# Two rows of conditioning stored another way, and a second, earlier call that makes the first layer's filter spectra

## The chip, the cores and the metric

The kernel runs on one core of a Trainium2 chip. The metric is the device time of one execution in microseconds (us); the median of three runs is compared. An execution is also recorded by the hardware profiler, and all rows below come from that one record.

## The reference, cut to what matters

Two layers of a diffusion backbone. Each layer mixes tokens in four head groups and then applies an MLP. What matters here is the start of the first layer:

```python
mx = modulation(c, ada_w[l], ada_b[l])        # silu(c) @ w + b, six vectors of 1024
mc = modulation(c_ctx, ada_w[l], ada_b[l])    # the same for the 256 context tokens
hx = rmsnorm(x, norm_pre_mix[l]) * (1.0 + mx[1]) + mx[0]
px = hx @ w_in[l]                             # 512 tokens; pc likewise for the context
h_fwd, h_bwd = hyena_filters(L, ...)          # needs weights alone, neither x nor c
y = irfft(rfft(u, n=2*L) * rfft(kern))        # long convolution with that filter, L = 512 and 256
```

The spectrum of the filter (`rfft(kern)`) and the sum of its absolute values depend on weights only. The reference needs each of them once per layer and length.

## The kernel before

All inputs lie in HBM. Almost every transfer is issued by SyncE's queue, SP, which issues in order: an instruction that waits holds all behind it. The order on each engine is fixed when the program is built, by a planner that takes the instructions of the source in turn and lets later ones go ahead where its own cost table finds the earlier ones not ready.

The start, in `run`, goes through these steps. `ccT` brings both conditioning vectors, features on partitions, and SiLU is applied to it. Two transfers store the vectors to a scratch tensor `cdr` in HBM, so that `cond_rows` can later read them back as rows on all 128 partitions (`cbc`). `first_scale` loads six blocks of 128 tokens (`X`, 512 KB each), squares and scales them. `mod_first` multiplies the vectors with four blocks of modulation weights, `adaP`: blocks 0 and 2 first (sixteen loads of 256 KB), blocks 1 and 3 inside the loop below (four loads of 1 MB). `first_turn` puts features on partitions. `filters` runs the small filter network. A loop over two halves of the features (`k0` is 0, then 4) applies the modulation in `first_norm` and gives `acth` and `actl`, the two parts of every main operand.

Then `mix` begins. `hyena_project` makes the main products of the first six blocks of `w_in` (lines 138 to 140; weights come as `raw` and are split into `whi` and `wlo`). Between them, `spectra_at` makes the filter spectra, length 512 ahead of the third block and length 256 ahead of the fifth:

```python
ld = {L: self.spectrum_loads(0, L, fp) for L in DFT_LENS}                            # L1589
self.fp, self.sp_in = fp, [(top[L == 256], ld[L], 0, L) for L in DFT_LENS]           # L1590
```

`spectrum` is a chain: products with the last filter weights (L465, TensorE), the window (L466, VectorE), absolute values (L467, ScalarE), one reduction over all of them (L469, VectorE), the sum and the difference of both directions (L472 and L473, GpSimd, into the buffer `ha` that the reduction has just read), the cosine and sine products (L508 for length 512, L521 for 256), their additions (L512 to L530, VectorE), the norm (L478 to L482) and a store of the spectrum to HBM (L484). The buffers `hw`, `ha`, `hw4`, `win`, `dft` exist once per length or once in all.

Of the kernel before, what the change touches and what calls it, by code (L numbers as in the profile page):

```python
# [9 lines left out]
F32 = mybir.dt.float32  # L10
# [35 lines left out]
class Net:  # L46
# [24 lines left out]
    def setup(self):  # L71
# [7 lines left out]
        # minus one on one block of 32 or 64 partitions  # L79
# [50 lines left out]
    def split(self, x, y, r):  # L130
        """x as two parts, into the columns r of the pair y."""
        self.nc.scalar.copy(y[0][:, r], x)
        self.nc.vector.tensor_sub(y[1][:, r], x, y[0][:, r].bitcast(F32))

    def mm3(self, o, st, mv, first, last):
        """o (+)= st.T @ mv with both operands as sums of two parts."""
        mmul = self.nc.tensor.matmul
        mmul(o, st[0], mv[0], start=first, stop=False)  # L138
        mmul(o, st[0], mv[1], start=False, stop=False)  # L139
        mmul(o, st[1], mv[0], start=False, stop=last)  # L140

    def pair(self):
        """Two banks of PSUM."""
        return self.pb.tile([128, 2, 512], F32, tag="pb", name="pb", bufs=3)

    def big(self, wsrc, acts, segs):
        """Products of one block of output features; returns a PSUM tile per token range."""
# [19 lines left out]
    def mod_first(self, p, i, act, cb=None):  # L167
        """One block of the shift (i < 2) or scale of the first norm. Few rows: four parts of the sum share the
        array's columns. The weights of some blocks lie where the normed activations will go."""
# [29 lines left out]
    def first_scale(self, XS, p):  # L199
        """Each block of 128 features of the input: features onto partitions, in place, with unit norms."""  # L200
# [39 lines left out]
    def cond_rows(self, p):  # L240
        """The activated conditioning vectors as rows on every partition."""
# [5 lines left out]
    def mod_steps(self):  # L247
        """One step per block of rows."""
# [19 lines left out]
    def ring(self, p, tag, bufs):  # L268
        """Where the blocks of modulation weights are loaded from now on."""
        self.row_block = lambda: p.tile([128, D], F32, tag=tag, name="adrow", bufs=bufs)  # L270
# [6 lines left out]
    def fac_pre(self, l, i, cnd, k0=0, k1=KB):  # L277
        """gain * (1 + m) of the norm before a sub-layer; i = 0 mixing, 1 mlp."""
# [4 lines left out]
    def fac_post(self, l, i, cnd, p):  # L283
        """gain * m of the norm after a sub-layer, as a row on every partition."""
# [21 lines left out]
    def post_norm(self, Y, row, X, out, p):  # L306
        """out = X + norm(Y) * gain * m for one block of tokens; returns what ends it, which returns a free buffer."""
# [14 lines left out]
    def finish(self, t, mm, ws, Y, row, X, p, before):  # L322
        """The last products and norm of one block of tokens, by halves of the features; before() ends the block
        before. Returns what ends this one."""
# [23 lines left out]
    def pre_scale(self, X, t, p):  # L348
        """The identity times the reciprocal norms."""
# [5 lines left out]
    def pre_norm(self, l, i, xs, p, out, off, cnd, dgs=None):  # L355
        """Features onto partitions; h = norm(x) * gain * (1 + m) + m' as two parts."""
# [59 lines left out]
    def filters(self, ld, p):  # L416
        """The filter networks up to their last hidden layer, two side by side on the partitions: both layers' of the
        long filter, and both halves of the short one's times."""
# [19 lines left out]
    def spectrum_loads(self, l, L, p):  # L438
        """What a filter's spectrum is made from."""
# [10 lines left out]
    def spectrum(self, hs, ld, l, L, p):  # L450
        """Spectrum of a two-sided filter at the odd frequencies and the norm of each channel."""
# [35 lines left out]
    def spectra(self, dft, uc, us, L, p, sp):  # L487
        """The cosine and sine sums over the even and odd times, E +- O, at the odd frequencies:
        [128 k, (C+, C-, S+, S-), k block, channel]. The frequencies of the second block mirror those of the first:
        there the sums over the times 1 and 3 modulo 4 trade cosines for sines, the others only signs."""  # L490
# [5 lines left out]
        if nk == 2:  # L496
            # (source, cosines or sines, parity, where the sum and the difference go)
# [39 lines left out]
    def hyena_project(self, l, w_in, hx, segs, p):  # L537
        """The convolved projections: x1 * v (two blocks) and x0 (two blocks)."""
# [21 lines left out]
    def hyena(self, l, u, x0, segs, ydst, p):  # L560
        nc, a = self.nc, self.a
        for off, L in segs:
# [43 lines left out]
            # the sums of both blocks that belong to each residue of the time: [(residue, cosine or sine)]  # L606
# [25 lines left out]
    def gdn_project(self, l, nm, j0, w_in, hx, segs, psum):  # L632
        """One of q, k and v: projected, convolved, activated and turned to tokens on partitions."""
# [18 lines left out]
    def gdn_rates(self, l, w_ab, hx, segs, p):  # L652
        """The logs of decay and beta, tokens on partitions. Few columns: four groups of them share the array,
        each with its part of the sum."""
# [27 lines left out]
        def rates(after):  # L682
# [6 lines left out]
            # log(1 + e) = log(w) + (e - (w - 1)) / w with w = fl(1 + e)  # L689
# [13 lines left out]
    def gdn_normalise(self, tok, p, rates):  # L703
        """Unit norm and rotary of keys and queries in place."""
# [44 lines left out]
    def gdn_solve(self, l, tok, la, lbeta, p, values):  # L749
# [3 lines left out]
        # feature-major q and k: [2 heads x 64, pair, tokens]  # L753
# [13 lines left out]
        # cumulative log decay, forward and backward, and the total of each block  # L767
# [47 lines left out]
    def gdn_systems(self, kT, qT, nq, p, ip):  # L815
        """Per direction, block and head: the system's strictly triangular part, transposed, and the query
        weights."""
# [35 lines left out]
    def gdn_inverse(self, UX, p, ip):  # L853
        """UX holds N (strictly triangular parts and a diagonal that is ignored); becomes (I + N)^-1."""
        nc = self.nc
        # the diagonal 32-blocks; slots without a system still pass through the 32 x 32 transposes
# [5 lines left out]
        for dr in range(2):  # L862
# [6 lines left out]
            # the blocks with rows before columns for the first direction, after for the second: both lower  # L869
            nc.vector.transpose(S[:, dr] if dr == 0 else S[:, dr].rearrange("p j i -> p i j"),  # L870
                                G[:, dr].rearrange("p u i -> p i u"))
        # the blocks between the halves go apart, zeros in their place and on the diagonal
# [9 lines left out]
        # substitution inside the 32-blocks, both directions at once  # L882
# [7 lines left out]
        # back: G[32 b + j, u, i] = T[i, j] and its transpose GT  # L890
# [11 lines left out]
    def gdn_levels(self, UX, G, GT, Xt, BB, ip):  # L902
        """From the inverses of the 32-blocks to those of 64 and of 128. Every sum runs over all partitions, with
        zeros in all but one block, which keeps the array at its full clock; the directions and blocks work on
        different columns of it at the same time."""
# [4 lines left out]
        def lower(zp, w, signs):  # L910
            """The products of one stage, negated; a part per block of partitions."""
# [11 lines left out]
        # 32 -> 64: block (a, b) of each pair  # L923
# [38 lines left out]
        # 64 -> 128  # L962
# [25 lines left out]
    def gdn_chain(self, dr, X, qk, ring, tok, seen, nq, p):  # L988
        """The blocks of one direction in turn; yields between stages, so that two directions can alternate.
        The sum of both directions takes the place of the queries."""  # L990
# [13 lines left out]
        def decayed(st):  # L1004
            """Keys and queries times their decay from the start of the block, features on partitions."""
# [109 lines left out]
    def na_project(self, w_in, hx, segs, full, dst):  # L1115
        """Queries and keys as two parts, and the values; one step per block of output features."""
# [26 lines left out]
    def na_heads(self, l, src, y, p, pn, with_ctx):  # L1143
# [7 lines left out]
        for pr in range(2):  # L1151
# [3 lines left out]
            # per head: both parts of the queries, and the keys' first part against each; the keys' second part  # L1155
            # lies with the queries' first
# [26 lines left out]
            for n in range(nq):  # L1183
# [40 lines left out]
                # the heads share the array's columns  # L1224
# [59 lines left out]
    def mix(self, l, hx):  # L1284
# [17 lines left out]
        with self.pool("tok") as self.tp:  # L1302
# [12 lines left out]
            with self.pool("gdn") as gp:  # L1315
# [9 lines left out]
                with self.pool("psg", 4, space=PSUM) as self.pg, self.pool("pso", space=PSUM) as self.po:  # L1325
                    na = self.na_project(w_in[14:20], hx, segs, full, nad)

                    def others(n):
                        """Work that fills the gaps of the inverse, and the values."""
# [28 lines left out]
    def mlp(self, l, ysp, ysp_s):  # L1358
# [7 lines left out]
        def runs(ts):  # L1366
            """Neighbouring tiles with the same modulation."""
# [177 lines left out]
    def run(self):  # L1545
# [11 lines left out]
        with self.pool("x0") as p:  # L1557
            self.cvec = p.tile([128, KB, 32], F32, tag="ccT", name="ccT")
            nc.sync.dma_start(self.cvec, a["ccT"])
            nc.scalar.activation(self.cvec, self.cvec, AF.Silu)  # L1560
            self.cdr = self.dp.tile([1, 2, D], F32, name="cdr", tag="cdr")
            for i in range(2):
                nc.sync.dma_start(self.cdr[0, i].rearrange("(k p) -> p k", p=128), self.cvec[:, :, i])
            fl = self.filter_loads(fp)

            XS = p.tile([128, NBLK, D], F32, name="X0", tag="X0")
            self.first_scale(XS, p)
            for i in (0, 2):
                self.mod_first_out(p, i, self.mod_first(p, i, True))
# [4 lines left out]
            for k0 in (0, 4):  # L1574
                for c in range(2):
                    self.fac_pre(0, 0, c, k0, k0 + 4)
                if k0 == 0:
                    ps = {i: self.mod_first(p, i, False, cb) for i in (1, 3)}
# [4 lines left out]
                if k0 == 0:  # L1583
                    for i in (1, 3):
                        self.mod_first_out(p, i, ps[i])
            nc.sync.dma_start(self.hsd, top[0][64:128])
# [47 lines left out]
def _blocks(w, nb):  # L1634
    """[K, N] -> [N / 128, 128, K / 128, 128]: one contiguous tile per block of outputs."""
# [4 lines left out]
def _layout(x, c, ctx, c_ctx, ada_w, ada_b, norm_pre_mix, norm_post_mix, norm_pre_mlp, norm_post_mlp,  # L1640
# [4 lines left out]
    A["ccT"] = np.pad(np.stack([c[0], c_ctx], -1), ((0, 0), (0, 30))).reshape(KB, 128, 32).transpose(1, 0, 2)  # L1645
    A["adaP"] = ada_w[0][:, :2 * D].reshape(2, 4, 128, 4, 512).transpose(3, 0, 2, 1, 4)
# [28 lines left out]
    # relative position bias, gathered for the queries (row, column) of a column block and its key window  # L1675
# [34 lines left out]
```

## Time and profile before

| what | value |
|---|---|
| median of three runs | 1896.51 us (1891.33 to 1897.97) |
| span of the profiled execution, first to last instruction | 1898.1 us |
| TensorE busy over the span | 1804.4 us, 95% |
| VectorE, ScalarE, GpSimd busy | 1269.1, 775.0, 256.7 us |
| moved by DMA | 233.54 MB, mean 123 GB/s |

The page gives no other time of the profiled execution than its span. Engines are PE (TensorE), PEld (its weight loads), DVE (VectorE), ACT (ScalarE), POOL (GpSimd) and SP. A row of a table by stretch reads: stretch, length, then for PE, PEld, DVE, ACT and POOL the busy time and in brackets the number of instructions, then the granted TensorE clock (1.00 is 2.4 GHz, 0.50 is 1.2 GHz), the busy share of the DMA engines and GB/s. A row of the timeline reads: start, duration, engine, line, operation, output<-input, shapes, count, and in square brackets the idle time before and what ended it. A row of a group reads: line, engine, operation, names, shapes, count, then busy us and mean ns, then idle us before it and what ended that. A row of DMA issues ends with KB each and the median us to landing.

### The profile page before, as it was taken

The page shows a single profiled execution, that of the slowest core. Times are in us where ns is not written, and L with a number is a line of the kernel's source. Part 1 is how long each engine was busy: PE and PEld are TensorE (multiplying, and loading weights), DVE is VectorE, ACT ScalarE, POOL GpSimd, SP SyncE. Part 2 cuts the span into 40 slices and gives each one's busy share as a digit, 9 for nine tenths or more (in the row PEclk, how much of TensorE's full clock was granted, in tenths as well). Part 3 has the DMA queues.
Part 4 walks back from the last instruction along what each step waited for, and adds up shares of the span by engine and source line. Part 5 has one row for each costly group of instructions (what it writes and reads, how often), then busy time and mean ns, then how long its engine had stood idle before and what let it go on. Part 6 is the DMA issues. An engine that isn't in the chain of part 4 may idle for free. (4 is left out here: it accounts for less than half of the span.)

```text
span 1898.1 us, 29470 instructions
## 1 busy us (share of the span) xinstructions
PE 1804.4 (95%) x11170; PEld 1450.4 (76%) x11170; DVE 1269.1 (67%) x2366; ACT 775.0 (41%) x1547; POOL 256.7 (14%) x265
## 2 busy tenths in 40 slices
PE   5899888999999999999999999998899999999998
PEld 2577777777779888888888876777676788777876
DVE  3888989665766777755555586779856665454545
ACT  4433553366556222222222263363346563332323
POOL 0202441500022000000000041152230110000002
PEclk9999999999999999999999999989999999999999
DMA  8452312344555434444434233112233664232322
GB/s 276 145 177 83 121 42 98 120 134 129 166 181 180 146 116 127 131 125 128 133 124 132 78 130 131 62 64 84 77 98 112 194 198 127 83 117 72 106 89 83
DMA packets 107073, 233.54 MB, mean 123 GB/s; under 512 B 14929, under 2 KB 19859, under 8 KB 105652
## 3 DMA queue, kind: packets, MB, share of 16 engines
q1 hardware_dynamic: 106932, 231.67, 38.7%
q8 instruction: 88, 1.44, 0.3%
q14 instruction: 53, 0.43, 0.1%
HBM read 208.41 MB, written 23.21 MB: 122 GB/s over the span
## 5 line engine op out<-in xcount | busy, mean ns | idle before, releaser
L126 ACT CAST whi<-raw 128x512 fp32r<-128x512 f32 x444 | 273.6, 620 | 671.6 <-PE pb L140 261.8
L127 DVE TENSOR_TENSOR wlo<-raw,whi 128x512 fp32r<-128x512 f32 x444 | 316.9, 720 | 215.9 <-ACT whi L126 209.7
L140 PE MATMUL pb<-acth,wlo 128*128 128x512 f32 (+2 forms) x808 | 282.6, 350 | 0.0
L139 PE MATMUL pb<-actl,whi 128*128 128x512 f32 (+2 forms) x808 | 282.2, 349 | 0.0
L138 PE MATMUL pb<-acth,whi 128*128 128x512 f32 (+2 forms) x808 | 281.4, 348 | 0.0
L138 PE MATMUL pb<-whi,hid 128*128 128x512 f32 x628 | 249.6, 397 | 0.1
L139 PE MATMUL pb<-wlo,hid 128*128 128x512 f32 x628 | 248.7, 396 | 0.5 <-DVE wlo L127 0.4
L140 PE MATMUL pb<-whi,hid 128*128 128x512 f32 x628 | 248.6, 396 | 0.0
L1497 DVE TENSOR_TENSOR acc<-acc,pb 128x1024 f32<-128x1024 f32 x96 | 117.2, 1221 | 150.5 <-PE pb L140 149.5
L258 DVE SCALAR_TENSOR_TENSOR junk<-adrow,cbc 128x512 bf16<-128x512 f32 x256 | 181.1, 707 | 5.1 <-DMA adrow<-in_adaD_dram 1.8
L139 PE MATMUL mx<-actl,whi 128*128 128x512 f32 x416 | 174.3, 419 | 1.4 <-POOL actl L374 1.1
L138 PE MATMUL mx<-acth,whi 128*128 128x512 f32 x416 | 170.3, 410 | 2.1 <-ACT acth L235 1.2
L140 PE MATMUL mx<-acth,wlo 128*128 128x512 f32 x416 | 171.7, 413 | 0.5 <-DVE wlo L127 0.4
L138 PEld LDWEIGHTS pb<-acth,whi 128*128 128x128 f32 x808 | 152.5, 189 | 20.3
L139 PEld LDWEIGHTS pb<-actl,whi 128*128 128x128 f32 x808 | 152.1, 188 | 20.1
L140 PEld LDWEIGHTS pb<-acth,wlo 128*128 128x128 f32 x808 | 152.5, 189 | 19.7
L374 POOL TENSOR_TENSOR actl<-et,acth 128x256 fp32r<-128x256 f32 (+2 forms) x64 | 56.1, 892 | 745.1 <-DVE et L373 740.4
L138 PEld LDWEIGHTS pb<-whi,hid 128*128 128x128 f32 x628 | 117.7, 187 | 32.4 <-ACT hid L1398 5.1
L140 PEld LDWEIGHTS pb<-whi,hid 128*128 128x128 f32 x628 | 117.8, 188 | 29.5 <-DVE hid L1399 1.8
L139 PEld LDWEIGHTS pb<-wlo,hid 128*128 128x128 f32 x628 | 117.8, 188 | 28.7 <-DVE wlo L127 1.6
L138 PEld LDWEIGHTS mx<-acth,whi 128*128 128x128 f32 x416 | 79.9, 192 | 20.1 <-ACT acth L235 1.6
L139 PEld LDWEIGHTS mx<-actl,whi 128*128 128x128 f32 x416 | 80.5, 194 | 19.1 <-POOL actl L374 1.8
(396 smaller groups left out, 3033.7 us busy)
## 6 DMA issues: line engine op xcount, KB each, us to landing
raw<-in_w_dram SPq DMA_DIRECT2D x276, 256.0 KB, 2.9
adrow<-in_adaD_dram SPq DMA_DIRECT2D x80, 512.0 KB, 3.7
raw<-in_win_dram SPq DMA_DIRECT2D x104, 256.0 KB, 2.8
raw<-in_wout_dram SPq DMA_DIRECT2D x64, 256.0 KB, 3.0
X<-xdr SPq DMA_DIRECT2D x14, 512.0 KB, 4.6
X<-in_xin_dram SPq DMA_DIRECT2D x12, 512.0 KB, 4.4
xdr<-X SPq DMA_DIRECT2D x10, 512.0 KB, 2.9
adp<-in_adaP_dram SPq DMA_DIRECT2D x16, 256.0 KB, 5.4
```

The costliest lines, as they stand in the source:

```text
L126: self.nc.scalar.copy(hi, raw)
L127: self.nc.vector.tensor_sub(lo, raw, hi.bitcast(F32))
L138: mmul(o, st[0], mv[0], start=first, stop=False)
L139: mmul(o, st[0], mv[1], start=False, stop=False)
L140: mmul(o, st[1], mv[0], start=False, stop=last)
L258: nc.vector.scalar_tensor_tensor(self.junk, raw[:, hs], 1.0, self.cbc[:, cnd, hs], op0=OP.mult, op1=OP.mult, accum_out=self.part[:, l, cnd ...
L374: nc.gpsimd.tensor_sub(lo[:, r], t, hi[:, r].bitcast(F32))
L1497: op = nc.vector.tensor_add(o, o, ps)
```

## The change

The two stores of `cdr` from `ccT`, whose access order `(k p) -> p k` writes single 4-byte elements, are taken out. A new input `ccF` holds the same vectors as 128 rows of 16 values (64 bytes); it is loaded, goes through SiLU, and is stored to `cdr` as 128 rows of 64 bytes, behind the six loads of `X`. The loads of the filter network come first.

In the loop, `spectrum_loads` for both lengths is called ahead of the loads of `adaP` blocks 1 and 3, and `spectrum` is called at the end of each half: length 512 after the first, 256 after the second. Lines 1589 and 1590 and the calls in `hyena_project` are not in the diff: they stay. The rest of the diff takes out comments and leaves blank lines.

```diff
             nc.scalar.activation(self.cvec, self.cvec, AF.Silu)
+            fl = self.filter_loads(fp)
             self.cdr = self.dp.tile([1, 2, D], F32, name="cdr", tag="cdr")
-            for i in range(2):
-                nc.sync.dma_start(self.cdr[0, i].rearrange("(k p) -> p k", p=128), self.cvec[:, :, i])
-            fl = self.filter_loads(fp)
+            flat = p.tile([128, 16], F32, tag="ccF", name="ccF")
+            nc.sync.dma_start(flat, a["ccF"])
+            nc.scalar.activation(flat, flat, AF.Silu)
 
             XS = p.tile([128, NBLK, D], F32, name="X0", tag="X0")
             self.first_scale(XS, p)
+            nc.sync.dma_start(self.cdr[0].rearrange("c (p j) -> (c p) j", j=16), flat)
...
                 if k0 == 0:
+                    ld = {L: self.spectrum_loads(0, L, fp) for L in DFT_LENS}
                     ps = {i: self.mod_first(p, i, False, cb) for i in (1, 3)}
...
                 if k0 == 0:
                     for i in (1, 3):
                         self.mod_first_out(p, i, ps[i])
+                L = DFT_LENS[k0 > 0]
+                self.spectrum(top[L == 256], ld[L], 0, L, fp)
             nc.sync.dma_start(self.hsd, top[0][64:128])
             self.cond_rows(cb)
             self.mods = self.mod_steps()
             ld = {L: self.spectrum_loads(0, L, fp) for L in DFT_LENS}
...
+    A["ccF"] = np.stack([c[0], c_ctx], 0).reshape(128, 16)
```

## Rows read from the trace of the kernel before

**Rows 1.** The page, busy time of each engine over the span.

```profile
PE 1804.4 (95%) x11170; PEld 1450.4 (76%) x11170; DVE 1269.1 (67%) x2366; ACT 775.0 (41%) x1547; POOL 256.7 (14%) x265
```

**Rows 2.** Table by stretch, the input loads (columns are explained above).

```profile
9.00:10.00 1.00, 0.07 (x2) 0.00 (x0) 0.67 (x2) 0.27 (x1) 0.00 (x0) 1.00 1.12 7
...
18.00:19.00 1.00, 0.00 (x0) 0.00 (x0) 0.76 (x4) 0.00 (x0) 0.00 (x0) 1.00 0.27 53
...
18.00:46.00 28.00, 21.35 (x86) 8.44 (x87) 13.38 (x35) 17.77 (x35) 0.00 (x0) 1.00 1.00 386
```

**Rows 3.** DMA view of 6 to 18 us: packets by size, and an issue.

```profile
DMA packets 2400, 0.99 MB, mean 83 GB/s; under 512 B 2112, under 2 KB 2112, under 8 KB 2400
...
cdr<-ccT SPq DMA_DIRECT2D x2, 4.0 KB, 11.0
```

**Rows 4.** Timeline of the first 65 us, ScalarE's rows.

```profile
20.86 1.06 ACT L206 ACTIVATE x0j<-X 128x1024 bf16<-128x1024 f32 x1 [4.15 <-DMA X<-in_xin_dram]
...
48.28 4.91 ACT L235 ACTIVATE acth<-X,mod,fac 128x512 fp32r<-128x512 f32 x8
...
62.11 4.90 ACT L235 ACTIVATE acth<-X,mod,fac 128x512 fp32r<-128x512 f32 x8 [7.38 <-DVE fac L280]
```

**Rows 5.** Table by stretch, from the turned input to the norm's end.

```profile
30.00:48.00 18.00, 17.35 (x87) 7.60 (x84) 10.16 (x26) 10.74 (x23) 0.00 (x0) 1.00 1.02 402
48.00:75.00 27.00, 23.56 (x133) 15.67 (x134) 20.07 (x41) 13.47 (x23) 7.51 (x8) 1.00 0.62 210
```

**Rows 6.** Timeline, products of the spectra at the full clock.

```profile
110.34 1.13 PE L465 MATMUL fps<-hw,hs 64*128 64x512 f32 x4
...
95.75 1.89 PE L508 MATMUL dps<-ha,dft 128*128 128x256 f32 x8
```

**Rows 7.** Groups between 75 and 128 us: the instructions of the spectra.

```profile
L508 PE MATMUL dps<-ha,dft 128*128 128x256 f32 x24 | 8.6, 502 | 3.9 <-POOL ha L472 3.0 <-POOL ha L473 0.8
...
L521 PE MATMUL dps<-ha,dft 128*128 128x256 f32 x8 | 4.1, 638 | 2.9 <-POOL ha L472 2.9
L478 PE MATMUL fps<-cst,hn 128*128 128x1 f32 x8 | 1.2, 252 | 0.0
...
L466 DVE TENSOR_TENSOR hw<-fps,win 128x512 f32<-128x512 f32 x6 | 4.0, 682 | 0.0
...
L481 DVE TENSOR_SCALAR inv<-fps 128x2 f32<-128x2 f32 x2 | 0.3, 148 | 0.0
...
L472 POOL TENSOR_TENSOR ha<-hw 128x1024 f32<-128x1024 f32 (+1 forms) x2 | 5.4, 2706 | 42.0 <-PE mx L138 26.3 <-DVE hn L469 15.7
L473 POOL TENSOR_TENSOR ha<-hw 128x1024 f32<-128x1024 f32 (+1 forms) x2 | 4.5, 2248 | 0.0
```

**Rows 8.** Table by stretch, around both spectra.

```profile
85.00:88.00 3.00, 0.03 (x1) 0.03 (x1) 3.00 (x3) 0.00 (x0) 2.80 (x2) 1.00 0.32 87
...
89.00:95.00 6.00, 5.19 (x14) 3.74 (x13) 5.45 (x10) 1.26 (x3) 1.67 (x1) 0.50 0.32 89
...
117.00:119.00 2.00, 0.00 (x0) 0.00 (x0) 1.97 (x5) 0.00 (x0) 2.00 (x1) 0.97 0.20 43
...
120.00:125.00 5.00, 5.00 (x12) 3.89 (x12) 2.28 (x8) 0.37 (x1) 1.33 (x1) 0.50 0.38 147
```

**Rows 9.** Timeline, the same VectorE subtraction without and beside GpSimd's sums.

```profile
59.77 1.28 DVE L127 TENSOR_TENSOR wlo<-raw,whi 128x512 fp32r<-128x512 f32 x2
...
85.04 6.17 DVE L127 TENSOR_TENSOR wlo<-raw,whi 128x512 fp32r<-128x512 f32 x3
```

**Rows 10.** Timeline of SP's queue from 30 to 70 us.

```profile
33.03 2.37 SPq L181 DMA_DIRECT2D adp<-in_adaP_dram  x4
...
59.15 0.33 SPq L245 DMA_DIRECT2D cbc<-cdr  x1
...
65.27 1.76 SPq L118 DMA_DIRECT2D raw<-in_win_dram  x3
```

**Rows 11.** DMA view of 0 to 80 us: modulation blocks 1 and 3.

```profile
adp<-in_adaP_dram SPq DMA_DIRECT2D x4, 1024.0 KB, 8.9
```

## The prediction

> **What bounds the kernel now.** First comes the page's list of busy times: TensorE is busy 95% of the span [rows 1]. The reader is to see that time can be won only where TensorE waits, starts late or runs at a lower clock, and that work added to TensorE anywhere else is paid in full. All that the change touches lies ahead of 137 us, so I read the table by stretch there. Before 30 us TensorE is nearly idle and the inputs set the pace; from 30 to 75 us it is busy 17.35 of 18 and 23.56 of 27 us [rows 5]; later it stops twice, for the filter spectra [rows 8]. The groups and the timeline then give prices. After 137 us nothing is edited; TensorE stays the bound there, so I carry every microsecond of the front to the end unchanged.
>
> **Part 1, the stores of the conditioning vectors.** From 9 to 19 us the DMA engines are busy but move almost nothing: ten rows of one microsecond, of which the first has 7 and the last 53 GB/s; together they moved some 0.3 MB [rows 2]. In that time 2112 packets under 512 bytes went through, 2048 of them the single elements of the two stores, which took 11.0 us to land [rows 3]. The input blocks lie in the same queue, and ScalarE's second square waits for its block until 20.86 us [rows 4]. Without the stores, 0.3 MB at the 386 GB/s of the later stream [rows 2] takes 0.8 us: 9.2 us are won. The new load and store have 256 packets; at ten microseconds for 2048 that is 1.2 us, of which the load, half, lies ahead of the inputs: 0.6 us. The store and its wait for SiLU stand behind the six loads; behind it in SP's queue are the sixteen weight loads, which wait for the stream anyway. The new SiLU is one small ScalarE instruction in a stretch in which ScalarE waits for data. I take 8.6 us, with 7 and 9.2 as ends. The first norm starts at 48.28 us [rows 4]; it should come that much earlier, since TensorE is packed from 30 us on [rows 5] and the weights that it reads ride in the same stream.
>
> **Part 2, the early spectra.** The diff adds a call and takes none away: lines 1589 and 1590 stay, and so do the calls among the main products. Every spectrum of the first layer is therefore made twice, and both old stops stay where they are. The added work, each instruction at its price:
>
> TensorE: four L465 products take 1.13 us and eight L508 products 1.89 us at the full clock [rows 6], so 0.28 and 0.24 us each. Twelve L465 make 3.4 us, 24 L508 5.7 us, the 8 of L521, the same shape, 1.9 us, and L478 1.2 us [rows 7]. Sum 12.2 us.
>
> VectorE: 13 groups from L466 with 4.0 us to L481 with 0.3 us [rows 7], in sum 18.6 us. GpSimd: 5.4 and 4.5, so 9.9 us [rows 7]. ScalarE gets the absolute values and the copies; it is busy 13.47 of 27 us from 48 to 75 us [rows 5], which hides them.
>
> DMA: eight loads of 2.1 MB in all, now ahead of modulation blocks 1 and 3; at 386 GB/s that is 5.4 us [rows 2]. Those blocks were issued from 33.03 us over 2.37 us [rows 10] and landed after 8.9 us [rows 11], so by about 45 us, but the second half of the norm that needs them came only at 62.11 us [rows 4], behind main products of the first half. The delay of 5.4 us is less than the lead: I cost it at nothing; without the lead it would be 5.4 us. The second set of loads refills buffers that the early set has to release, behind `cbc`, which was issued at 59.15 us [rows 10]; there is no work between that they could hold up but the `raw` weights, below.
>
> What hides the 12.2 us? TensorE's free time from 48 to 75 us, 27 less 23.56, so 3.4 us [rows 5]; 8.8 us are left. If all of it is used and the 0.65 us free between 30 and 48 as well, 8.1 us; if none, 12.2 us.
>
> New waits: the products L508 need GpSimd's sums, and these the long reduction. At the old places TensorE stood still for 3.0 us, later 0.8 us, and 2.0 us in the second table row for this, and after it the clock stood at 0.50, which is 1.2 GHz, for 5.2 and 5.0 us of work, half of which, 5.1 us, is loss [rows 8]. That bounds the early waits between nothing and 10.9 us. The early place has a less loaded VectorE, 20.07 of 27 us against 3.00 of 3 and 5.45 of 6 at the old one [rows 5, 8], so the reduction should come sooner; I take the shorter of the two plain waits, 2.0 us.
>
> SP's queue: the early stores of the spectra wait for the end of their chains, and refills and then the `raw` weights stand behind them. Before, three of these were issued at 65.27 us [rows 10], with the weights of the first two blocks long loaded. I take nothing, with 5.4 us, the time of one set of refills, as the other end.
>
> Sum along TensorE: -8.6 + 8.8 + 2.0 = +2.2 us. Sum along VectorE: it has 6.9 us free from 48 to 75 us [rows 5], so -8.6 + 18.6 - 6.9 = +3.1 us. The two run side by side and the longer one counts: +3 us. From the profiled span of 1898.1 us that is 1901.1 us. The median of the runs stands 1.6 us below the span, so I forecast 1899.5 us: no change that can be told.
>
> **The rivals.**
>
> *The old stop twice (slower).* The place is the wait of L508 and L521 for GpSimd at the end of each half of the norm. If main products of the first half are used up by then, TensorE has nothing to put in between, and both stops with their low clock come again: -8.6 + 8.8 + 10.9 = +11.1 us, 1907.6 us. It decides once more than some 9 of the 10.9 us return. For it: in the old place there were main products ready and the fixed order still stopped. Against it: from 48 to 75 us the clock stayed at 1.00 despite short waits [rows 5].
>
> *VectorE becomes the bound (slower).* Beside GpSimd's sums, three subtractions took 6.17 us where two took 1.28 [rows 9], so 4.2 us more; the sums of the long filter, over half of the 9.9 us, took some 5.5. In the early place the norm's own subtractions lie beside 9.9 us of them: 4.2 x 9.9 / 5.5 = 7.6 us, and +3.1 + 7.6 = +10.7 us, 1907.2 us. It decides once the norm's second half waits for the stretched instructions. Against it: the planner may put the sums beside other work. The Trainium skill (GPSIMD Engine Reference, Key points) says that GpSimd shares its SBUF interfaces with VectorE and contends with VectorE instructions that have two SBUF inputs; the stretched subtraction is one, and no rule there says how much is lost.
>
> *All hidden (faster).* If the planner spreads the early set over TensorE's waits before and inside the norm, and the norm of the second half stays where the weights put it, only part 1 is left: -8.6 us, 1887.9 us. Against it: only some 4 us are free on TensorE [rows 5].
>
> *Only one set is run (faster).* Nothing reads the early spectra; if the later set were the one to go when the program is built, the old stops would go too: -8.6 - 3.4 - 10.9 = -22.9 us, 1873.6 us. The source calls both, so this is unlikely.
>
> **How the numbers follow.** A measurement of this kernel tells some 0.5%, 9.5 us, from no change. Forecast 0.60 (all of it within), the old stop twice 0.15, VectorE 0.09, all hidden 0.10 (half beyond the bound), only one set 0.06. So faster 0.05 + 0.06 = 0.11, slower 0.24, same 0.65. The range goes from just below the all-hidden case, 1887 us, to 1910 us, 2 us above the slower cases for `raw` weights that come late; it leaves out the one-set case and the worst sums of several.
>
> **What would show it.** Right for part 1: no stretch near zero GB/s between 9 and 19 us, the second square at about 11 to 12 us, the first norm near 40 us. Right for part 2: 48 L508 products from `ha` instead of 24 in the first layer, and the last main product of the third block at nearly the old time. Wrong if the first norm starts less than 7 us earlier (something else sets the start), if the L508 count stays 24, if the clock shows 0.50 ahead of 70 us (old stop twice), or if the old stops shrink or grow in their unchanged place, which no step above foresees.

## The result and the profile after

The changed kernel takes 1916.01 us (median of 4 runs, 1910.92 to 1922.22) against 1897.24 us before (4 runs): ratio 1.0109, 95% interval 1.0082 to 1.0136. It is 1.1% slower, clear of the noise, and 6 us above the range. The profiled execution's span is 1915.4 us against 1898.1, so 17.3 us longer.

The page of the changed kernel, busy times, answers to [rows 1]: TensorE is busy 19.6 us longer, part of it at the lower clock, with 52 more instructions.

```profile
PE 1824.0 (95%) x11222; PEld 1461.5 (76%) x11222; DVE 1285.3 (67%) x2396; ACT 783.2 (41%) x1562; POOL 264.8 (14%) x269
```

Part 1 did what was said. In the changed kernel's table by stretch, the second that showed 7 GB/s in [rows 2] now moves 299:

```profile
9.00:10.00 1.00, 0.50 (x4) 0.10 (x2) 0.27 (x1) 1.00 (x3) 0.00 (x0) 1.00 0.83 299
```

and in its timeline ScalarE's second square stands at 12.03 us, not 20.86 [rows 4]:

```profile
12.03 1.06 ACT L206 ACTIVATE x0j<-X 128x1024 bf16<-128x1024 f32 x1 [0.94 <-DMA X<-in_xin_dram]
```

What went wrong can be seen in the timeline of the changed kernel from 38 to 79 us; its rows L235 answer to [rows 4]:

```profile
39.64 1.12 PE L465 MATMUL fps<-hw,hs 64*128 64x512 f32 x2
...
40.59 0.81 ACT L235 ACTIVATE acth<-X,mod,fac 128x512 fp32r<-128x512 f32 x1 [0.20 <-DVE fac L280]
...
49.07 1.98 PE L465 MATMUL fps<-hw,hs 64*128 64x512 f32 x4
50.98 1.92 PE L184 MATMUL modps<-adp,ccT 128*32 128x512 f32 x16
52.47 3.61 DVE L469 TENSOR_REDUCE hn<-ha 128x256 f32<-128x2048 f32 x1 [0.69 <-ACT ha L467]
56.16 2.34 POOL L472 TENSOR_TENSOR ha<-hw 128x1024 f32<-128x1024 f32 x1 [8.04 <-DVE hn L469]
...
58.56 2.07 PE L508 MATMUL dps<-ha,dft 128*128 128x256 f32 x4 [5.66 <-POOL ha L472]
60.86 2.93 PE L508 MATMUL dps<-ha,dft 128*128 128x256 f32 x6 [0.23 <-POOL ha L473]
63.71 1.41 PE L184 MATMUL modps<-adp,ccT 128*32 128x512 f32 x8
65.05 0.66 PE L194 MATMUL modt<-cst,adrow 128*128 128x128 f32 x4
65.54 1.46 PE L508 MATMUL dps<-ha,dft 128*128 128x256 f32 x6
66.93 1.07 PE L184 MATMUL modps<-adp,ccT 128*32 128x512 f32 x8
67.93 1.99 PE L508 MATMUL dps<-ha,dft 128*128 128x256 f32 x8
...
70.00 0.63 PE L194 MATMUL modt<-cst,adrow 128*128 128x128 f32 x4
...
73.93 4.91 ACT L235 ACTIVATE acth<-X,mod,fac 128x512 fp32r<-128x512 f32 x8 [3.60 <-DVE fac L280]
```

The first half of the norm starts at 40.59 us, 7.7 us earlier. The second starts at 73.93, 11.8 us later than its 62.11. It needs the modulation products L184 and their turns L194. Half of those products ran at 50.98; the other half stand in TensorE's fixed order behind the first spectrum products L508, which wait for GpSimd's sum L472, and that for the reduction L469. Their weights had landed by then: the stretches from 53 to 65 us below show 0 GB/s.

The changed kernel's table by stretch shows four such stops where [rows 8] had two, each followed by work at a granted clock near 0.5, which is 1.2 GHz (after the fourth the clock is back at 1.00 from 143 us on, so that row's mean is 0.76):

```profile
53.00:58.50 5.50, 0.00 (x0) 0.00 (x0) 3.68 (x2) 0.00 (x0) 2.34 (x2) 0.92 0.00 0
58.50:65.00 6.50, 6.22 (x18) 3.22 (x18) 1.51 (x4) 0.75 (x2) 2.30 (x2) 0.54 0.00 0
...
84.20:87.50 3.30, 0.09 (x1) 0.00 (x0) 3.30 (x4) 0.88 (x2) 1.32 (x2) 1.00 0.97 325
87.50:95.00 7.50, 6.94 (x26) 6.00 (x27) 3.35 (x9) 2.30 (x5) 1.18 (x1) 0.56 0.09 36
...
109.00:112.50 3.50, 0.57 (x4) 0.14 (x2) 3.50 (x3) 1.00 (x2) 2.42 (x2) 0.96 0.01 2
112.50:119.00 6.50, 5.82 (x13) 4.20 (x14) 3.92 (x10) 0.74 (x2) 2.68 (x1) 0.50 0.27 81
...
136.00:141.00 5.00, 2.11 (x8) 1.41 (x6) 3.94 (x8) 0.20 (x1) 4.28 (x2) 0.85 0.49 161
141.00:145.00 4.00, 4.00 (x15) 3.06 (x13) 2.07 (x7) 0.76 (x3) 0.09 (x1) 0.76 0.17 65
```

In the groups of the changed kernel from 38 to 156 us the spectra's products of [rows 7] are there twice:

```profile
L508 PE MATMUL dps<-ha,dft 128*128 128x256 f32 x48 | 17.0, 500 | 9.5 <-POOL ha L472 8.6 <-POOL ha L473 0.9
...
L465 PE MATMUL fps<-hw,hs 64*128 64x512 f32 x24 | 11.6, 628 | 0.0
L521 PE MATMUL dps<-ha,dft 128*128 128x256 f32 x16 | 6.9, 550 | 6.7 <-POOL ha L472 6.1 <-ACT odd L524 0.6
...
L478 PE MATMUL fps<-cst,hn 128*128 128x1 f32 x16 | 2.5, 257 | 0.0
```

Behind the main products of these blocks, 48 of each kind with 512 columns from 38 us on here and in e1 below, comes the turn of the convolution's input (L576, `utps`). It starts at 136.77 us before and 155.29 after: 18.5 us of loss are made by then, and 17.3 are left at the end of the profiled execution.

### The profile page after: what moved, and what is told of

It reads as the page before. It is cut to its first block, busy times and chain, and to the rows that moved or that the text cites. A ratio compares the mean times of both kernels' runs of the same rounds, so it can differ in the third digit from the quotient of the medians.

```text
span 1915.4 us, 29658 instructions
## 1 busy us (share of the span) xinstructions
PE 1824.0 (95%) x11222; PEld 1461.5 (76%) x11222; DVE 1285.3 (67%) x2396; ACT 783.2 (41%) x1562; POOL 264.8 (14%) x269
## 5 line engine op out<-in xcount | busy, mean ns | idle before, releaser
L127 DVE TENSOR_TENSOR wlo<-raw,whi 128x512 fp32r<-128x512 f32 x444 | 312.9, 710 | 209.9 <-ACT whi L126 205.4
L1497 DVE TENSOR_TENSOR acc<-acc,pb 128x1024 f32<-128x1024 f32 x96 | 117.3, 1222 | 153.5 <-PE pb L140 152.4
L139 PEld LDWEIGHTS mx<-actl,whi 128*128 128x128 f32 x416 | 80.4, 193 | 18.4 <-POOL actl L374 1.9
```

The costliest lines, as they stand in the source:

```text
L127: self.nc.vector.tensor_sub(lo, raw, hi.bitcast(F32))
L1497: op = nc.vector.tensor_add(o, o, ps)
```

## The experiments

Eleven kernels ran. "Early" is the set of spectra that the change adds, "late" the old one. The account beside the times is TensorE's from 38 us to the turn L576: time in which it stood still, and what its work lost at the lower clock (busy time times the missing share of the clock, summed over stretches of 1 us); the rest is work at the full clock. It comes from one profiled execution of each kernel. At 38 us the kernel before and e2 stand at the same place. The kernels with part 1 are some 8 us of work further on and lie within about 2 us of one another: 5 to 13 products L220 and 8 to 12 turns L194 are still to come. The last products L184 of blocks 0 and 2 start at 35.24 to 36.83 us there, and e8 at 35.24, e1 at 35.42 and the changed kernel at 36.63 show that this is not a matter of the early loads alone. So differences of 1 to 2 us at L576 say little. Each ratio is taken against runs of the kernel before made together with it; the result, e1 to e4, e5 to e8 and e9 to e11 are separate groups, and between groups the ratios compare better than the medians.

| kernel | median us | ratio to before (95%) | L576 at us | still | clock loss | work |
|---|---|---|---|---|---|---|
| before | 1897.2 | 1 | 136.8 | 11.1 | 6.0 | 81.7 |
| after | 1916.0 | 1.0109 (1.0082 to 1.0136) | 155.3 | 18.4 | 10.5 | 88.4 |
| e1 stores only | 1886.4 | 0.9966 (0.9949 to 0.9983) | 126.8 | 11.2 | 4.2 | 73.4 |
| e2 spectra only | 1923.0 | 1.0152 (1.0125 to 1.0179) | 162.2 | 19.4 | 8.9 | 95.9 |
| e3 moved | 1888.1 | 0.9967 (0.9951 to 0.9982) | 127.9 | 11.5 | 4.2 | 74.2 |
| e4 modulation first | 1907.6 | 1.0072 (1.0046 to 1.0099) | 149.4 | 14.8 | 8.9 | 87.7 |
| e5 early loads | 1889.5 | 0.9971 (0.9954 to 0.9988) | 127.5 | 11.2 | 4.4 | 73.9 |
| e6 moved, modulation first | 1885.5 | 0.9952 (0.9938 to 0.9966) | 123.1 | 8.3 | 3.1 | 73.7 |
| e7 early 512 | 1908.4 | 1.0077 (1.0057 to 1.0097) | 148.4 | 18.4 | 7.4 | 84.6 |
| e8 early 256 | 1910.1 | 1.0077 (1.0051 to 1.0102) | 141.6 | 15.3 | 12.1 | 76.1 |
| e9 two parts | 1911.3 | 1.0079 (1.0047 to 1.0111) | 152.9 | 13.3 | 10.8 | 90.7 |
| e10 moved, two parts | 1881.8 | 0.9923 (0.9898 to 0.9947) | 125.1 | 8.7 | 3.4 | 75.0 |
| e11 stores, two parts | 1891.0 | 0.9963 (0.9945 to 0.9981) | 124.6 | 9.4 | 2.8 | 74.3 |

### e1 and e2: each part alone

e1 takes the early loads and the early calls out of the changed kernel:

```diff
-                    ld = {L: self.spectrum_loads(0, L, fp) for L in DFT_LENS}
...
-                L = DFT_LENS[k0 > 0]
-                self.spectrum(top[L == 256], ld[L], 0, L, fp)
```

Expected: 

> Part 1 of the change alone: the stores as 64-byte rows behind the input loads, filter loads first; no early spectra and no early loads of theirs. Every theory expects the first norm's first half 7 to 9 us earlier than in the kernel before (it stood at 48.28 us, after the change at 40.59). If the front loss comes all from part 2, the second half of the norm comes 7 to 9 us earlier too (before 62.11, so 53 to 55) and the whole kernel is about 8 us shorter than before: about 1889 us, ratio to before 0.995 to 0.996. If the gain of part 1 is lost downstream anyway (the rows of after wander between +10 and +18.6 us between 160 and 1900 us), the time stays within 3 us of before.

e2 adds just these lines to the kernel before, and keeps its element-wise stores. Expected: 

> Part 2 alone: the early loads and early spectra as in the changed kernel, but the vectors stored as before, element by element. The two parts add up if they meet nowhere: then 1916 + 8 = about 1924 us, ratio to before about 1.014. If the products of the early spectra stand in TensorE's fixed order ahead of the last modulation products and only the reduction's end counts (which does not depend on the norm of the first half, but on the filter weights and VectorE), the later input takes away part of that stop and the loss shrinks: 1916 to 1920 us.

In e1 the halves of the norm move by 8.8 and 8.7 us (timeline):

```profile
39.48 4.90 ACT L235 ACTIVATE acth<-X,mod,fac 128x512 fp32r<-128x512 f32 x8
...
53.38 4.91 ACT L235 ACTIVATE acth<-X,mod,fac 128x512 fp32r<-128x512 f32 x8 [7.45 <-DVE fac L280]
```

Its ratio is worth 6.4 us (3.2 to 9.7). e2 costs 1.52%, or 28.8 us. The two parts add up: -6.4 + 28.8 = +22 beside the +20.7 of the change (both by ratio). Everything lost comes from part 2. Between e1 and the changed kernel the turn L576 moves by 28.5 us: 15.0 of work, 7.1 of standing still, 6.3 at the lower clock. Some 1.2 of the 15.0 are products that e1 has behind it at 38 us. Between the kernel before and e2, which start level, it moves by 25.4 us: 14.2, 8.3 and 2.9.

### e3: made once, early

```diff
-            ld = {L: self.spectrum_loads(0, L, fp) for L in DFT_LENS}
-        self.fp, self.sp_in = fp, [(top[L == 256], ld[L], 0, L) for L in DFT_LENS]
+        self.fp, self.sp_in = fp, []
```

Expected: 

> The changed kernel with the late loads and the late calls of the first layer's spectra taken out: each spectrum is made once, early. Theory 'duplicate work': the loss is the twelve microseconds of TensorE and the stops at the old place; both go, and the kernel ends at 1916 - 12.2 - 6 to 11 = 1893 to 1898 us or, with part 1's gain in full, 1889. Theory 'order' (the last modulation products stand behind the early products of the spectrum on TensorE): the second half of the norm still starts near 74 us instead of 62, TensorE still stands still for 5 us from 53 us on at a low clock afterwards, and the kernel keeps some 12 us of loss less the 12 + 6 us taken out beside it: 1896 to 1902 us. The two are told apart by the start of the second half of the norm: below 65 us for the first, above 70 us for the second.

The norm's second half still starts at 73.19 us, and the waits of TensorE in the first 165 us are the long ones:

```profile
PE dps L508 <- POOL ha L472: 5.7, 1, 5.7
...
PE dps L521 <- POOL ha L472: 3.5, 1, 3.5
```

Yet the time is that of e1, and L576 comes only 1.1 us later than there. So taking out the second set gives back 27.4 us at L576, more than the 18 to 23 us of the first theory, and its time, 1888.1 us, is that theory's 1889; the late norm is the sign of the second. Moving the spectra as such is worth nothing either way: the two early stops (5.7 and 3.5 us) stand in place of the late ones (3.0 and 2.9 us), and in all TensorE stands still for 11.5 and 11.2 us, with 4.2 us of clock loss in both. That the late norm does no harm is not shown by this: e6 below gains 4.7 us at L576 over e3 with an earlier one.

### e4: the modulation products first

Both sets stay; only TensorE's order changes (`mod_first_out` returns its last turn):

```diff
-                        self.mod_first_out(p, i, ps[i])
+                        turned = self.mod_first_out(p, i, ps[i])
...
-                self.spectrum(top[L == 256], ld[L], 0, L, fp)
+                with self.tc.issue_after(turned.ins):
+                    self.spectrum(top[L == 256], ld[L], 0, L, fp)
```

Expected: 

> The changed kernel with everything made twice as in it, but on TensorE the early spectrum's instructions may come only behind the last turn of modulation blocks 1 and 3; no other edit. Theory 'order': the second half of the norm starts at 54 to 60 us instead of 73.93, the still stand of 5.5 us from 53 us on is filled by main products or goes, and the kernel is 8 to 13 us shorter than the changed one: 1903 to 1908 us. Theory 'duplicate work' (the twelve microseconds and the stops count wherever they stand): the norm comes early, but the same work and the same stops follow later, and the time stays within 3 us of 1916. Theory 'early loads' (2.1 MB ahead of the modulation weights delay them): the second half of the norm stays above 68 us.

The timeline, with line numbers one higher:

```profile
48.70 2.78 PE L184 MATMUL modps<-adp,ccT 128*32 128x512 f32 x24
...
53.91 0.66 PE L194 MATMUL modt<-cst,adrow 128*128 128x128 f32 x4 [0.81 <-DVE adrow L191]
57.77 1.29 ACT L236 ACTIVATE acth<-X,mod,fac 128x512 fp32r<-128x512 f32 x2
...
67.36 1.32 PE L509 MATMUL dps<-ha,dft 128*128 128x256 f32 x4 [3.39 <-POOL ha L473]
```

The second half of the norm starts 16.2 us earlier, though in pieces, the wait for GpSimd falls from 5.66 to 3.39 us, and 5.9 us are won at L576 (3.6 of stillness, 1.6 of clock). This is a net figure. In the changed kernel products L465 stand at 39.64 and 41.06 us, while the first norm is made; here they come only at 54.49 us, TensorE waits 1.2 us for the norm instead, and its clock is low until 47 us, some 3 us of clock loss that the changed kernel does not have. The time, 8.4 us lower (7.0 by the ratios), is where the order theory put it; the intervals of the two ratios overlap. At L576 the order is a part of the loss, about a fifth of the 28.5 us; the rest is the second set.

### e5: the early loads alone

The early calls go, their loads stay, and nothing reads them:

```diff
-                L = DFT_LENS[k0 > 0]
-                self.spectrum(top[L == 256], ld[L], 0, L, fp)
```

Expected: 

> The changed kernel with the early calls of the spectra taken out but their eight loads of 2.1 MB kept ahead of the loads of modulation blocks 1 and 3 (nothing reads what they bring; the late set is loaded and made as before). Theory 'the loads are free' (the modulation weights have a lead over the second half of the norm): the same as the stores alone, 1886 us within 3 us, and the second half of the norm at 53 to 55 us. Theory 'early loads' (they delay the modulation weights, or the weights behind them in SP's queue): the second half of the norm 3 to 5 us later than that, 56 to 59 us, and 1890 us or more.

```profile
48.61 2.78 PE L184 MATMUL modps<-adp,ccT 128*32 128x512 f32 x24
...
56.03 4.90 ACT L235 ACTIVATE acth<-X,mod,fac 128x512 fp32r<-128x512 f32 x8 [6.16 <-DVE fac L280]
```

In the timeline the norm's second half comes 2.65 us later than in e1, because these products now start at 48.61 us instead of 40.78. That is inside the window named for delayed weights; TensorE shows no wait for them there, so whether the weights or the planner's order put the products back is open. But L576 moves by 0.7 us and the time by nothing that can be told: 1889.5 us falls between the two theories, and the ratios are 0.9971 and 0.9966. The loads are not the cause of the loss.

### e6: made once, early, modulation first

The edits of e3 and e4 together. Expected: 

> Each spectrum made once, early, and on TensorE only behind the last turn of modulation blocks 1 and 3. With the spectra made twice the same order brought the first long-convolution product 5.9 us forward. Theory 'order counts by itself': about 4 to 6 us shorter than the moved kernel at 1888 us, so 1882 to 1884 us and the shortest of all. Theory 'only the second set counts' (moving alone was 1.1 us from the stores alone at the first long-convolution product, though its norm came 20 us later than theirs, so the norm's second half does not set the pace when the main products still have other work): within 2 us of 1888.

L576 comes 4.7 us earlier than in e3, as the order theory said, but of that 2.6 us are left in the medians, 1885.5 against 1888.1, with overlapping intervals of the ratios, and 1885.5 lies outside both windows. The first theory holds at L576; at the end the two are not told apart.

### e7 and e8: one early length each

```diff
-                self.spectrum(top[L == 256], ld[L], 0, L, fp)
+                if L == 512:
+                    self.spectrum(top[L == 256], ld[L], 0, L, fp)
```

and `if L == 256` in e8. Expected for length 512: 

> The changed kernel with only the early spectrum of length 512 (all early loads kept, the late set kept whole). By the account of TensorE's time from 38 us to the first long-convolution product, the early set cost 28.5 us there against the stores alone: 15.0 of work, 7.2 of standing still, 6.3 of work at the lower clock. Theory 'the account is additive': two thirds of the work, and the stop of 5.7 us with its low clock, so 17 to 20 us behind the stores alone, 1903 to 1906 us, with the second half of the norm still near 74 us. Theory 'two calls disturb each other': less than 14 or more than 23 us.

Expected for length 256: 

> The changed kernel with only the early spectrum of length 256 (all early loads kept, the late set kept whole). Theory 'additive': the rest of the 28.5 us, 8 to 12 us behind the stores alone, 1894 to 1898 us; the second half of the norm is back at 53 to 55 us, since no product of a spectrum stands ahead of the last modulation products; the wait of 3.2 us for GpSimd and the lower clock behind it, seen at 84 to 95 us after the change, are still there some 20 us earlier. If instead the loss of the early set was made by the late norm alone, this kernel is within 3 us of the stores alone, 1886 us.

e7 comes a little above the 17 to 20 us that the additive account gave: 21.6 us behind e1 at L576, 21 in time by the ratios, the norm's second half at 73.85 us. e8 is far above its 8 to 12 us: 14.8 us behind at L576 and also 21 in time, and the second half of its norm starts at 67.27 us, not at 53 to 55. Its timeline shows what the front costs more:

```profile
49.54 1.07 PE L184 MATMUL modps<-adp,ccT 128*32 128x512 f32 x8
52.92 1.13 PE L521 MATMUL dps<-ha,dft 128*128 128x256 f32 x4 [2.31 <-POOL ha L472]
54.60 2.05 PE L521 MATMUL dps<-ha,dft 128*128 128x256 f32 x4 [0.55 <-ACT odd L524]
56.58 1.94 PE L184 MATMUL modps<-adp,ccT 128*32 128x512 f32 x8
```

The expectation that nothing stands ahead of the modulation products was wrong: with only length 256 early, its L521 takes the place that L508 had, though the source calls it behind the second half of the norm. The products behind it take 1.94 us for eight instead of 1.07, since the clock stays at 0.50 from 55 to 64 us. Of e8's clock loss some 3 us lie ahead of its spectrum, from 40 to 48 us, where e1 has none. Another 10 us are lost against e1 between 236 and 420 us, in and around the inverse, where nothing is edited; there the waits list has a row that e1 lacks:

```profile
PE tp L945 <- issue: 5.2, 1, 5.2
```

Why this stage came out slower was not settled. The loss of single early lengths is not additive: 21.6 + 14.8 against 28.5.

### e9 to e11: a shorter chain

In each spectrum the reduction and the two sums are done by halves of the time blocks, and the norm's product L478 adds the two parts:

```diff
-        nc.vector.tensor_reduce(hn, ha.rearrange("p t d c -> p c (t d)"), axis=AX.X, op=OP.add)
...
+        for r in range(2):
+            s = slice(r * nt // 2, (r + 1) * nt // 2)
+            nc.vector.tensor_reduce(hn[:, r], ha[:, s].rearrange("p t d c -> p c (t d)"), axis=AX.X, op=OP.add)
...
+            nc.gpsimd.tensor_add(ha[:, s, 0, :], hw[:, s, 0, :], hw[:, s, 1, :])
+            nc.gpsimd.tensor_sub(ha[:, s, 1, :], hw[:, s, 0, :], hw[:, s, 1, :])
```

e9 is the changed kernel with that, e10 is e6 with it, e11 is e1 with it. Expected for e9: 

> The changed kernel, every spectrum still made twice, but in each spectrum the reduction and GpSimd's two sums are done in two parts, by halves of the time blocks, so that behind the last absolute values only half a reduction and half a sum stand ahead of the first products (the norm's product adds the two parts: eight more small products per layer and length pair). Theory 'the stop is as long as the chain': behind the last absolute value stood 3.61 us of reduction and 2.34 us of sum for length 512, 1.95 and 1.26 us for length 256, in halves 3.0 and 1.6 us less; the two early stops and the two old ones (8.6 and 6.1 us of waits) lose 7 to 9 us together, with some of the lower clock behind them: 1903 to 1909 us. Theory 'the old stops are set by VectorE's queue' (busy 4.9 of 5 us there): only the early ones shrink, by 3 to 5 us: 1911 to 1913 us. If the place of the products in TensorE's order matters and not the chain's length, the time stays within 3 us of 1916.

Expected for e10: 

> Each spectrum made once, early, behind the modulation blocks, with the reduction and sums in two parts. Theory 'the stop is as long as the chain': from the 1885.5 us of the same kernel without the parts, the waits for GpSimd of 3.4 and 0.6 us go for the most part, and their lower clock with them (3.1 us of loss ahead of the first long-convolution product): 1880 to 1883 us. If these waits are covered or come back elsewhere, within 2 us of 1885.5.

Expected for e11: 

> The stores alone (no early spectra), with the reduction and sums in two parts. Theory 'the stop is as long as the chain': the two old stops, 3.0 and 2.9 us of waits and 4.2 us of lower clock, shrink by 4 to 7 us: from 1887 us to 1880 to 1883. Theory 'the old stops are set by VectorE's queue': within 2 us of 1887.

The waits of e9 in the first 165 us:

```profile
PE dps L512 <- POOL ha L474: 4.8, 4, 2.1
PE dps L525 <- POOL ha L474: 3.6, 4, 1.3
...
PE dps L512 <- POOL ha L475: 1.5, 3, 0.5
...
PE dps L525 <- ACT odd L528: 0.5, 1, 0.5
```

Together 10.4 us, against 16.2 in the changed kernel (8.6, 6.1, 0.9 and 0.6): the stops are in part as long as the chain. But L576 gains only 2.4 us: standing still shrinks by 5.1, work grows by 2.3 (the added small products among it) and the lower clock stays, and 1911.3 is not told from 1916.0. In e11 L576 comes 2.2 us earlier than in e1, but nothing is won in the time: 1891.0 beside 1886.4, and ratios of 0.9963 and 0.9966. e10 has the lowest median, 1881.8, as the chain theory said, but at L576 it stands 2 us later than e6, so its gain isn't shown to come from the shorter chain. It is 0.77% faster than before (0.53% to 1.02%), the lowest ratio of all versions; its interval overlaps e6's.

## Why the prediction was wrong

**Part 1: right.** The sum took 8.6 us off; the first norm came 7.7 us earlier in the changed kernel and 8.8 in e1. The 1.1 us between the two are there ahead of the early set: the last products L184 of blocks 0 and 2 stand at 36.63 us in the one and at 35.42 in the other, within the spread of the kernels with part 1 (35.24 to 36.83). At L576 e1 is 10.0 us ahead of the kernel before, 8.3 by the earlier start and 1.8 by less work at the lower clock. The time shows 6.4 us (3.2 to 9.7).

**The work of the early set: 12.2 us predicted, about 14 measured** (14.2 from the kernel before to e2; 15.0 from e1 to the changed kernel, less the 1.2 named above). The L465 term was mis-sized. All twelve were priced by a row of four in 1.13 us [rows 6]. That row is of length 256; the eight of length 512 took 4.15 us in one row of the kernel before, 0.52 each instead of 0.28:

```profile
75.49 4.15 PE L465 MATMUL fps<-hw,hs 64*128 64x512 f32 x8
```

In the changed kernel the L465 group grew by 6.4 us, not 3.4: the early four of length 256 were dear too, since they ran two by two with main products between. The first pair in its timeline:

```profile
72.87 1.12 PE L465 MATMUL fps<-hw,hs 64*128 64x512 f32 x2
```

In the code the two time blocks of length 256 use different halves of the partitions, those of length 512 the same half. The Trainium skill (TensorEngine Tiling (Array Packing), Tiling Modes) lists two row tiles of 64 for such operands; two at a time would fit the trace: a product of the code is two instructions here, and four side by side, both halves, took 1.13 us, two alone 1.12. No run here changed the halves.

**The cover: 3.4 us predicted, none found.** This and the next step failed. TensorE's free time between 48 and 75 us was counted as room for the added work. It is not room: the order is fixed, and a product with a late operand holds all behind it. Standing still grew by 7.1 us instead of shrinking.

**The early waits: 2.0 us predicted, without any clock loss.** They were 5.66 and 0.23 us for length 512 and 3.2 for 256, and the lower clock took 6.3 us more. The reason given, a less loaded VectorE, was no help: VectorE sat idle for 0.69 us ahead of the reduction, waiting for ScalarE's `ha`, and then the chain of 3.61 us of reduction and 2.34 us of sum is serial. What counts is what TensorE has to do meanwhile: in e4 it has main products left, and waits 3.39 us. The value taken was also a short reading: the stretch of 2.0 us in [rows 8] ends before the wait does, which [rows 7] give as 2.9 us. The bound of 10.9 us for these stops was nearer than the value taken, and still too low: 7.1 + 6.3 = 13.4 us.

**The norm's second half.** The prediction looked for the arrival of the modulation weights and found a lead. That was right for the weights, which were there, and blind for the products, of which half went behind L508. e4 prices the order at 5.9 us net at L576; 3.6 and 1.6 of it come back from the 7.1 and 6.3.

**The sum.** At L576: -10.0 (e1) + 15.0 + 7.1 + 6.3 = +18.4 us (18.5 measured), where the prediction had -8.6 + 8.8 + 2.0 along TensorE. The +3 that it forecast came from the sum along VectorE, which did not set the pace: over the span VectorE was busy 16.2 us longer, and from 38 us to L576 it was busy 90.1 of 117.3 us.

**The rivals.** "The old stop twice" named the mechanism: a stop and 1.2 GHz ahead of 70 us, and again after it. Its price, 1907.6 us, was 8 us short, by the work and by the cover that it kept. "Only one set is run" is out: 48 products L508. "All hidden" is out. That VectorE becomes the bound is not shown: it was busy 3.68 of the 5.5 us of the first stop, with the reduction that TensorE's chain waited for. That the old stops stay where they are among the main products held: they are there at 109 and 136 us, with waits of 2.9 us each where 3.0 and 2.9 stood. SP's queue: the raw weights of 65.27 us [rows 10] were issued at 82.48, and no wait of TensorE for them shows.

**After 137 us** the front's loss was to be carried unchanged. Over the profile it is 18.5 us at L576, 10 to 18 in between and 17.3 at the end, one execution beside one, but e8 shows that an edit at the front can move 10 us in an unedited stage.

## What to carry to other kernels

An engine's free time hides added work only if that work has its operands when its turn in the fixed order comes; look first for what stands behind a late operand, not for how much idle time there is. When a computation is moved ahead, check in the group counts that the old one is gone: the copy left behind cost 27 us at L576, and the move itself about nothing. Price an instruction from rows of its own shape and operands, since one line can hold two kinds.

## What the runs showed of the hardware

The clock loss was larger than the stops let expect. In e8 TensorE stood still for only 2.3 us, and for 0.55 us soon after, and then it was busy all of 9 us at half the clock (table by stretch):

```profile
50.60:52.90 2.30, 0.01 (x1) 0.00 (x0) 0.93 (x1) 0.00 (x0) 1.29 (x2) 1.00 0.00 0
...
55.00:58.00 3.00, 3.00 (x12) 0.85 (x11) 1.06 (x3) 1.31 (x4) 0.00 (x0) 0.50 0.00 0
58.00:61.00 3.00, 3.00 (x16) 1.13 (x12) 1.02 (x3) 0.62 (x2) 0.00 (x0) 0.50 0.66 218
61.00:64.00 3.00, 3.00 (x16) 0.92 (x12) 0.36 (x2) 0.00 (x0) 0.00 (x0) 0.50 0.00 0
```

The Trainium skill (TensorE: Matmul & The Clock Gate, HAM oscillation) describes this for waits for a DMA: the work behind them starts again at the lower clock, and half the time spent there is lost. The trace agrees, behind waits for GpSimd and ScalarE: eight L184 took 1.94 us there and 1.07 at 1.00.

What a stop costs beyond its own length is not fixed. Behind the same wait for the first norm, 1.17 us in e1 and 1.18 in e8, the clock stayed up in e1 and was low in e8 (tables by stretch, first e1, then e8):

```profile
41.00:47.00 6.00, 5.88 (x34) 3.11 (x27) 5.79 (x10) 4.93 (x9) 3.73 (x4) 1.00 0.26 74
...
41.00:47.00 6.00, 5.55 (x16) 3.51 (x15) 5.00 (x9) 3.22 (x6) 3.53 (x4) 0.50 0.97 371
```

What decided between them is not shown. Over the early set, 6.3 us at the lower clock came with 7.1 us of standing still between e1 and the changed kernel, and 2.9 with 8.3 between the kernel before and e2.
